# The first feed-forward layer of an encoder layer in two stages, with seven block products for eight

## The chip, the core and the metric

The kernel runs on one core of a Trainium2 chip. The metric is the device time in microseconds (us) of one execution. Three runs of the kernel before took 2439.05, 2436.93 and 2439.96 us, so the median is 2439.05 us. PE is the matrix engine, PEld its weight loads, DVE the vector engine, ACT the activation engine, POOL the general engine, SP the engine whose queue issues the transfers.

## The reference

One layer works on 1280 tokens of width 1024 in fp32: 256 of a prompt and 1024 of a sample.

```python
def swiglu(h, w_gu, w_down):
    gate, up = jnp.split(h @ w_gu, 2, axis=-1)
    return (jax.nn.silu(gate) * up) @ w_down

x = x + 0.5 * rms_norm(swiglu(rms_norm(x, ffn1_pre_g), ffn1_w_gu, ffn1_w_down), ffn1_post_g)
x = x + rms_norm(mixer(rms_norm(x, mix_pre_g), w_in, ..., w_out), mix_post_g)
x = x + 0.5 * rms_norm(swiglu(rms_norm(x, ffn2_pre_g), ffn2_w_gu, ffn2_w_down), ffn2_post_g)
x = rms_norm(x, final_g)
```

`w_gu` is 1024 x 5632 (gate and up of 2816 columns each), `w_down` is 2816 x 1024. The mixer (a projection `w_in`, dilated attention, a depthwise convolution, `w_out`) is not touched by the change.

## The kernel before, in words

**Tiles.** Tokens stand in ten blocks of 128: 0 to 7 are the sample, 8 and 9 the prompt. Blocks are grouped in three tiles (`TILES`, L27): t=0 and t=1 of 512 tokens, t=2 of 256. The normed tokens are kept transposed in `hT[t]`, as a high and a low fp32r part (`hTth`, `hTtl`); every weight is split likewise by an ACT copy and a DVE subtraction (`whi`/`wlo` at L90 and L91, `wb` at L114 and L115, `wd` and `ahl` at L637 and L638). `mm3` (L196 to L200) makes one product out of three matmuls: high x high, high x low, low x high. So all matmuls bear the lines L198, L199 and L200, and are told apart by their tiles. The 2816 hidden columns are 22 slices f of 128.

**First layer** (`ffn`, L340, names `psgu`, `ah`, `al`, `psd`, `y`). For each f and each tile, `gu` (L344) makes gate and up: 2 x 8 x 3 matmuls into two banks `psgu`, then silu and product (L370, L371) and the split of the result into `ah` and `al` (L372, L373). `dn` (L376) multiplies that slice with its 128 rows of `w_down` at once: 2 x 3 matmuls for each block, and DVE adds the two banks `psd` to the block's sum `y` in SBUF (L390; for f=0 ACT copies, L388). The last two slices go through `dn2` (L393, adds at L407). The matmuls of f=0 are cut into chunks of 256 tokens.

**Second layer** (from L1281; `ffn_gu` L488, `ffn_down` L597). Stage one: slices 0 and 1 as before (`gu`, L496), the remaining 20 by `pair` (L518). There gate and up of the sample are one 2 x 2 block product (gate and up on one side, the two halves of the contraction on the other, two tiles on the third), made of seven block products in place of eight (`for i in range(8)`, L528; the eighth step belongs to the prompt alone, in bank `psR`): 7 x 4 x 3 matmuls of 512 tokens into the banks `psAB` and `psC`, and 4 x 4 x 3 of 256 for the prompt. Its weights are sums of weight blocks (`Pairs`, L99: POOL adds at L134 to L140, then the split), and its tokens are sums of `hT` blocks (`token_sums`, L440: tiles `T2` to `T4`, and the first half of `hT1` overwritten), made once by DVE during slices 0 and 1. The gated activations `ac` go to DRAM (`ad`, L494). Stage two: `ffn_down` reads them back (`ar`, L620), splits them, and works in segments of (1, 3, 3, 3, 3, 3, 2, 4) slices: for each of ten blocks the matmuls of all slices of the segment run into `psd`, and the sum is added to the block (L667) once a segment (first segment: copies, L663 and L665). Weights of `w_down` are `wd`, loaded into the tag `g`.

**Behind each layer** the `chain` (L234) runs for each block in five steps, one at each call of `step` (L284): the sum of squares (ACT L206, POOL L207 and L208), scaling (DVE L212) and the residual (POOL L254), spill to DRAM (L263) and the second sum of squares, scaling (DVE L212 into `tmp`), transposes (PE L223) and the split into `hT` (ACT L225, DVE L226). For the first layer it feeds `w_in` (L684), whose first products are `psa`, `psb` (two column groups for each tile: 24 matmuls of each for a tile) and, behind them, `psqk`.

**Order.** Each engine works its queue in order. The order of the program is set by a scheduler that places the instructions by a time model, so that work of neighbouring steps is interleaved; all transfers are issued from SP's queue. Rings of buffers are set by tags: ten buffers `w` of 4 KB for split weights (L1197), two `raw`, two each of `x`, `tmp`, `g`, four PSUM banks of tag `g`, two double banks of tag `d`.

Of the kernel before, what the change touches and what calls it, by code (L numbers as in the profile page):

```python
# [10 lines left out]
F32 = mybir.dt.float32  # L11
# [87 lines left out]
class Pairs:  # L99
# [5 lines left out]
    def load(self, f, s):  # L105
        if f < NF and (f, s) not in self.raw:
            raw = self.t.wp.tile([P, D], F32, name="raw", tag="raw", bufs=2)
            c = s * FF + f * P
            self.t.nc.sync.dma_start(raw.rearrange("p (k m) -> p k m", k=KT), self.wgu[:, :, c:c + P])
            self.raw[f, s] = raw  # L110
# [38 lines left out]
class Trunk:  # L149
# [157 lines left out]
    def first(self, y, gname):  # L307
        nc = self.nc
        g = []
        V = {}  # L310

        def load(b0, b1):
            for b in range(b0, b1):
                nc.sync.dma_start(y[b], self.rows(self.a["x_prompt"], self.a["x_sample"], b))

        def s1(b):
            V[b] = self.rstd(y[b], self.tmp("tmp" if b % 2 else "x"), 1.0)

        def s2(b):
            self.scaled(y[b], y[b], V.pop(b), g[0])  # L320

        def s3(b):
            self.to_hT(b, y[b])

        load(0, 2)
        g.append(self.gain(gname))
        load(2, 4)
        return load, (s1, s2, s3)


    def ffn_units(self, w_gu, w_down):
        wgu = w_gu.rearrange("(k p) f -> p k f", p=P)
        units = []
        for f in range(NF):
            units.append((wgu[:, :, f * P:(f + 1) * P], (KT, P), None))
            units.append((wgu[:, :, FF + f * P:FF + (f + 1) * P], (KT, P), None))
            units.append((w_down[f * P:(f + 1) * P, :], (D,), None))
        return units

    def ffn(self, pool, S, base, y, done, prep=None, order=(0, 1, 2)):  # L340
        nc = self.nc
        act = {}

        def gu(f, t):  # L344
            n = TILES[t][1] * P
            if f == 0:
                self.ensure(t)
            hh, hl = self.hT[t]
            ps = []
            for s in range(2):  # L350
                o = self.bank("psgu")
                wh, wl = (z.rearrange("p (k m) -> p k m", k=KT) for z in S.w[base + 3 * f + s])
                for c0 in range(0, n, 256 if f == 0 else n):
                    c = slice(c0, c0 + 256 if f == 0 else n)
                    for k in range(KT):
                        self.mm3(o[:, c], (wh[:, k], wl[:, k]), (hh[:, k, c], hl[:, k, c]), k == 0, k == KT - 1)
                ps.append(o)
                if s == 0 or t < 2:
                    self.step()
            S.conv_to(base + 3 * f + 4 + t)  # L360
            tag = "c" if t == 2 else ""
            s = pool.tile([P, 512], F32, name="sg", tag="sg", bufs=1)
            if f == NF - 1:
                tag = ""
            if f == NF - 1 and t == 0:
                ah, al = self.tmp("x", (P, n), F32R), self.tmp("tmp", (P, n), F32R)
            else:
                ah = pool.tile([P, n], F32R, name="ah", tag="ah" + tag, bufs=1 if tag else 2)
                al = pool.tile([P, n], F32R, name="al", tag="al" + tag, bufs=1 if tag else 2)
            nc.scalar.activation(s[:, :n], ps[0][:, :n], AF.Silu)  # L370
            nc.vector.tensor_tensor(s[:, :n], s[:, :n], ps[1][:, :n], op=OP.mult)  # L371
            nc.scalar.activation(ah, s[:, :n], AF.Copy)  # L372
            nc.vector.tensor_tensor(al, s[:, :n], ah.bitcast(F32), op=OP.subtract)  # L373
            act[f, t] = ah, al

        def dn(f, t):  # L376
            dh, dl = S.w[base + 3 * f + 2]
            ah, al = act.pop((f, t))
            b0, nb = TILES[t]
            for j in range(nb):  # L380
                o = self.two_banks("psd")
                bl = slice(j * P, (j + 1) * P)
                for h in range(2):
                    c = slice(h * 512, (h + 1) * 512)
                    self.mm3(o[:, c], (ah[:, bl], al[:, bl]), (dh[:, c], dl[:, c]), True, True)
                yb = y[b0 + j]
                if f == 0:
                    nc.scalar.activation(yb, o, AF.Copy)  # L388
                else:
                    nc.vector.tensor_tensor(yb, yb, o, op=OP.add)  # L390


        def dn2(f, t):  # L393
            d = [S.w[base + 3 * g + 2] for g in (f - 1, f)]
            x = [act.pop((g, t)) for g in (f - 1, f)]
            b0, nb = TILES[t]
            for j0 in range(0, nb, 2):
                o = [self.two_banks("psd") for _ in range(2)]
                for i in range(2):
                    for j in range(2):  # L400
                        bl = slice((j0 + j) * P, (j0 + j + 1) * P)
                        for h in range(2):
                            c = slice(h * 512, (h + 1) * 512)
                            self.mm3(o[j][:, c], (x[i][0][:, bl], x[i][1][:, bl]), (d[i][0][:, c], d[i][1][:, c]), i == 0, i == 1)
                for j in range(2):
                    self.step()
                    nc.vector.tensor_tensor(y[b0 + j0 + j], y[b0 + j0 + j], o[j], op=OP.add)  # L407

        L = NF - 1
        for f in range(L):  # L410
            if f == 3 and prep:
                prep()
            if f == 0 and order[0] == 2:
                for t in order:
                    gu(0, t)
                dn(0, 0)
                dn(0, 1)
                continue
            gu(f, 0)
            if f:  # L420
                dn(f - 1, 2)
            gu(f, 1)
            if f < L - 1:
                dn(f, 0)
            gu(f, 2)
            if f < L - 1:
                dn(f, 1)
        for t in range(3):
            gu(L, t)
            dn2(L, t)  # L430
            done(t)

# [53 lines left out]
    def ffn_gu(self, pool, tpool, S, W, ad, orders, prep=None):  # L488
# [79 lines left out]
        def post(f, t, z, s):  # L568
            n = 2 * f + 3 + (z > 0)
            if n <= len(S.units):  # L570
                S.conv_to(n)
            elif z or s:
                W.to(1 if first else 3)
            if t == 1 and not T:
                t_, a_, b_ = self.token_sums(tpool)
                T.update(t_)
                first.extend(a_)
                then.extend(b_)
            if first:
                first.pop(0)()  # L580
            elif then and 1 in gone:
                then.pop(0)()
# [11 lines left out]
            pair(f)  # L594


    def ffn_down(self, ad, w_down, segs):  # L597
        nc = self.nc
        X, Wd, raw = {}, {}, {}
        c0 = [sum(segs[:s]) for s in range(len(segs) + 1)]  # L600
# [43 lines left out]
        def go(y, done):  # L644
            n0 = npre
            for s, n in enumerate(segs):
# [3 lines left out]
                for b in range(NB):  # L650
                    t = min(b // 4, 2)
                    k = n0 + -(-(n1 - n0) * (b + 1) // NB)
                    conv_to(k)
                    o = self.two_banks("psd")
                    j = (b - TILES[t][0]) * P
                    for c in cs:
# [525 lines left out]
def run(self):  # L1182
# [9 lines left out]
    def pool_(name, **kw):  # L1192
        m = tc.tile_pool(name=name, reuse_waits="tile", **{"bufs": 1, **kw})
        p = m.__enter__()
        return p, lambda: m.__exit__(None, None, None)

    wp, wp_x = pool_("wp", bufs=10, side="right")  # L1197
    self.wp = wp
    units = self.ffn_units(a["ffn1_w_gu"], a["ffn1_w_down"])
    b_in = len(units)  # L1200
    units += self.w_in_units()
    S = Stream(self, units)

    fy, fy_x = pool_("fy")
    fa, fa_x = pool_("fa", side="right")
    y = [fy.tile([P, D], F32, name=f"y{b}") for b in range(NB)]
    load, self.stages = self.first(y, "ffn1_pre_g")
    self.ready = list(range(NB))
    S.load_to(2)
    load(4, NB)  # L1210
    for _ in range(4):
        self.step()
    S.conv_to(1)
    self.ensure(0)
    S.conv_to(2)
    gp = self.gain("ffn1_post_g")
    gn = self.gain("mix_pre_g")

    def done1(t):
        if t == 0:  # L1220
            self.stages = self.chain(lambda b: y[b], xin, 0.5, gp, gn, spill=x2d)
        self.ready += range(TILES[t][0], sum(TILES[t]))

    def prep():
        z = self.tmp("tmp", (16, AW))
# [10 lines left out]
            nc.tensor.transpose(ps[:, j * (CK + 3):(j + 1) * (CK + 3)], cw[:, j * P:(j + 1) * P], self.ident[:CK + 3, :CK + 3])  # L1236
        nc.vector.tensor_copy(cv.rearrange("p j k -> p (j k)"), ps[:, 0:4 * (CK + 3)])

    self.ffn(fa, S, 0, y, done1, prep)
    fa_x()  # L1240
    wg, wg_x = pool_("wg", side="right")
    L = {}

# [3 lines left out]
        L["wc"], L["wc_x"] = pool_("wc")  # L1247
        return L["wc"]

    cacc = self.w_in(wg, conv_pool, S, b_in, qd, kd, vd, cv)  # L1250
    wg_x()
    wp_x()
    for t in range(3):
# [64 lines left out]

    self.place = place
    pre, go = self.ffn_down(ad, a["ffn2_w_down"], (1, 3, 3, 3, 3, 3, 2, 4))  # L1320
    self.ffn_gu(fa, ft, S2, Pairs(self, a["ffn2_w_gu"], 2, pre), ad, ((2, 0, 1), (1, 0, 2)))
    ft_x()
    fa_x()
    pools["p"], p_x = pool_("p2")
# [45 lines left out]
```

## Time and profile before

| | |
|---|---|
| median of three runs | 2439.05 us (2436.93 to 2439.96) |
| the profiled execution's own time | 2438.86 us |
| its span, first to last instruction | 2437.1 us |
| mean granted clock of PE over the span | 0.982 |
| DVE, ACT, POOL busy | 52%, 30%, 20% |
| first layer: first gate matmul, last down matmul | 18.1, about 949 us |
| second layer: first gate matmul, last down matmul | 1555.3, 2417.6 us |
| moved by DMA | 194.92 MB, mean 80 GB/s |

The span is the time from the first to the last instruction, and some 1.8 us of the execution lie around it. In the rows of the profile, a group is one line of the code with its output and input tiles, `x352` is the count, then come the busy time and the mean duration in ns. [...] In a row of the timeline, the number in brackets is how long the engine stood idle before it, with what ended the wait.

### The profile page before, as it was taken

The numbers are of one execution on the slowest core, as the hardware profiler recorded it, in microseconds if no ns is written. First come the engines' busy times: TensorE is split into PE (matmuls) and PEld (weight loads), VectorE is DVE, ScalarE is ACT, GpSimd is POOL, SyncE is SP. The second block draws the span as 40 slices with busy tenths as digits, with TensorE's granted clock in tenths as the row PEclk, the third lists the DMA queues.
The fourth block names the chain that finished last, engine by engine and source line by source line (L and its number), as shares of the span: only waits on it lengthen the run. The fifth ranks groups of instructions, "written<-read, shape, count | busy, mean of one in ns | idle before, by whom it ended". The sixth has DMA issues, their size and how long they took to land.

```text
span 2437.1 us, 30173 instructions
## 1 busy us (share of the span) xinstructions
PE 2350.7 (96%) x12028; PEld 2009.4 (82%) x12028; DVE 1263.2 (52%) x1695; ACT 739.9 (30%) x1387; POOL 491.5 (20%) x474
## 2 busy tenths in 40 slices
PE   7999999999999998999997799999999999999996
PEld 7888888888888887888886678888888888788885
DVE  5344444444444438899455553564344444454557
ACT  5211111111111125565356552332322222312113
POOL 2000000000000016797202233223232323100004
PEclk9999999999999999999998899999999999999998
DMA  5111111111111115241267552211222222432324
GB/s 179 44 35 44 35 44 35 44 35 44 35 44 35 44 61 164 70 124 61 78 157 148 112 157 95 93 57 61 72 70 68 74 62 84 130 106 68 106 74 154
DMA packets 191827, 194.92 MB, mean 80 GB/s; under 512 B 30212, under 2 KB 154916, under 8 KB 191686
## 3 DMA queue, kind: packets, MB, share of 16 engines
q1 hardware_dynamic: 191686, 193.00, 26.8%
q8 instruction: 94, 1.54, 0.3%
q14 instruction: 47, 0.39, 0.1%
HBM read 149.23 MB, written 43.73 MB: 79 GB/s over the span
## 4 chain that ended last, share of the span: by engine, by line
PE 87%; DMA 5%; DVE 3%; ACT 2%; issue 1%; POOL 1%; SPq 1%; POOLq 0%; ACTq 0%; DVEq 0%
PE psgu L198 9%; PE psgu L199 9%; PE psgu L200 9%; PE psd L198 7%; PE psd L199 7%; PE psd L200 7%; PE psAB L198 4%; PE psAB L199 4%; PE psAB L200 4%; PE psR L199 2%; PE psR L200 2%; PE psR L198 2%; PE psC L198 2%; PE psC L199 2%; PE psC L200 1%; PE psqk L198 1%
## 5 line engine op out<-in xcount | busy, mean ns | idle before, releaser
L390 DVE TENSOR_TENSOR y<-y,psd 128x1024 f32<-128x1024 f32 x190 | 231.6, 1219 | 176.2 <-PE psd L200 176.2
L207 POOL TENSOR_SCALAR st<-st 128x1 f32<-128x1 f32 x70 | 41.7, 596 | 1253.4 <-ACT tmp L206 981.8
L371 DVE TENSOR_TENSOR sg<-sg,psgu 128x512 f32<-128x512 f32 (+1 forms) x66 | 39.5, 599 | 273.0 <-PE psgu L200 273.0
L198 PE MATMUL psd<-wd,ahl 128*128 128x512 f32 x440 | 172.1, 391 | 3.3 <-DVE yh0l L663 1.4
L199 PE MATMUL psd<-wd,ahl 128*128 128x512 f32 x440 | 171.3, 389 | 0.0
L200 PE MATMUL psd<-wd,ahl 128*128 128x512 f32 x440 | 171.2, 389 | 0.0
L198 PE MATMUL psd<-whi,ah 128*128 128x512 f32 x432 | 169.7, 393 | 0.8 <-DVE y L407 0.8
L199 PE MATMUL psd<-wlo,ah 128*128 128x512 f32 x432 | 169.3, 392 | 0.0
L200 PE MATMUL psd<-whi,al 128*128 128x512 f32 x432 | 167.7, 389 | 0.0
L90 ACT ACTIVATE whi<-raw 128x1024 fp32r<-128x1024 f32 x98 | 103.2, 1058 | 212.1 <-PE psgu L199 166.9
L198 PE MATMUL psgu<-hT0h,whi 128*128 128x512 f32 (+1 forms) x416 | 155.9, 375 | 0.0
L198 PE MATMUL psgu<-hT1h,whi 128*128 128x512 f32 (+1 forms) x416 | 155.3, 373 | 0.5 <-ACT hT1h L225 0.5
L199 PE MATMUL psgu<-hT0l,whi 128*128 128x512 f32 (+1 forms) x416 | 155.6, 374 | 0.0
L200 PE MATMUL psgu<-hT0h,wlo 128*128 128x512 f32 (+1 forms) x416 | 155.4, 374 | 0.0
L91 DVE TENSOR_TENSOR wlo<-raw,whi 128x1024 fp32r<-128x1024 f32 x98 | 126.6, 1296 | 55.0 <-ACT whi L90 51.6
L199 PE MATMUL psgu<-hT1l,whi 128*128 128x512 f32 (+1 forms) x416 | 155.0, 373 | 0.0
L200 PE MATMUL psgu<-hT1h,wlo 128*128 128x512 f32 (+1 forms) x416 | 155.0, 373 | 0.0
L115 DVE TENSOR_TENSOR wb<-raw,wb 128x512 fp32r<-128x512 f32 x120 | 84.8, 708 | 106.4 <-ACT wb L114 103.9
L114 ACT ACTIVATE wb<-raw 128x512 fp32r<-128x512 f32 x120 | 75.5, 629 | 167.4 <-PE psC L200 68.0
L744 DVE SCALAR_TENSOR_TENSOR acc<-glu,cv,acc 128x1024 f32<-128x1024 f32 x96 | 121.5, 1284 | 1.8
L372 ACT ACTIVATE ah<-sg 128x512 fp32r<-128x512 f32 (+1 forms) x65 | 35.9, 553 | 253.0 <-DVE sg L371 253.0
L198 PE MATMUL psgu<-hT2h,whi 128*128 128x256 f32 x384 | 109.5, 286 | 2.8 <-DVE hT1l L226 2.8
(356 smaller groups left out, 6124.5 us busy)
## 6 DMA issues: line engine op xcount, KB each, us to landing
raw<-in_ffn_w_gu_dram SPq DMA_DIRECT2D x88, 512.0 KB
raw<-in_ffn_w_down_dram SPq DMA_DIRECT2D x22, 512.0 KB
ad<-ac SPq DMA_DIRECT2D x44, 256.0 KB
g<-in_ffn_w_down_dram SPq DMA_DIRECT2D x22, 512.0 KB
ar<-ad SPq DMA_DIRECT2D x44, 256.0 KB
raw<-in_w_in_dram SPq DMA_DIRECT2D x20, 512.0 KB
x2d<-y SPq DMA_DIRECT2D x10, 512.0 KB
q<-qd SPq DMA_DIRECT2D x16, 320.0 KB
```

The costliest lines, as they stand in the source:

```text
L90: nc.scalar.activation(hi, raw, AF.Copy)
L91: nc.vector.tensor_tensor(lo, raw, hi.bitcast(F32), op=OP.subtract)
L114: nc.scalar.activation(out[:, 0], src, AF.Copy)
L115: nc.vector.tensor_tensor(out[:, 1], src, out[:, 0].bitcast(F32), op=OP.subtract)
L198: mm(out, lh[0], rh[0], start=first, stop=False, skip_group_check=more)
L199: mm(out, lh[0], rh[1], start=False, stop=False, skip_group_check=more)
L200: mm(out, lh[1], rh[0], start=False, stop=last, skip_group_check=more)
L207: nc.gpsimd.tensor_scalar(st[:, 0:1], st[:, 0:1], 1e-6 / (mul * mul), None, op0=OP.add)
L371: nc.vector.tensor_tensor(s[:, :n], s[:, :n], ps[1][:, :n], op=OP.mult)
L372: nc.scalar.activation(ah, s[:, :n], AF.Copy)
L390: nc.vector.tensor_tensor(yb, yb, o, op=OP.add)
L744: nc.vector.scalar_tensor_tensor(V["acc"], gs(k), w(k), V["acc"], op0=OP.mult, op1=OP.add)
```

## The change

The first layer is computed by the functions of the second one. `ffn` and `ffn_units` are gone; `ffn_gu` and `ffn_down` are called for both layers. What differs from their use in the second layer:

- The prompt's blocks 8 and 9 are loaded first, and `gu(0, 2)` is the first product; tokens are loaded in the order 8, 9, (gain), 0, 1, then the first two weight slices, then blocks 2 to 7.
- Stage one has the tokens' tiles `y0` to `y9` in a pool `fy0` that is closed when the token sums are allocated (`tpool()`), so that `T2` to `T4` take their memory. The sums `y1` of stage two are in a new pool `fy`.
- The split `w_down` slices of a segment lie in the memory of `hT0` and `hT1` (free after stage one), in turn in two sets; of the last four slices, two lie in a pool `p1` and two in the memory of `hT2` (`where`, `place1`).
- `prep` (the convolution's constants) runs at the second pair.
- `also1` is called at each block of each segment: it loads the two gains after the last block but one segment, and in the last segment's blocks 7 to 9 loads and splits the first weights of `w_in`, which are now a stream of their own (`S_in`). `done1` appends each block to the chain at once in the last segment.
- The ring `w` has nine buffers.

```diff
-    def ffn(self, pool, S, base, y, done, prep=None, order=(0, 1, 2)):
...
-        load(0, 2)
+        load((8, 9))
         g.append(self.gain(gname))
-        load(2, 4)
+        load((0, 1))
...
-    def ffn_down(self, ad, w_down, segs):
+    def ffn_down(self, ad, w_down, segs, also=lambda s, b: None):
...
                     conv_to(k)
+                    also(s, b)
...
-    wp, wp_x = pool_("wp", bufs=10, side="right")
+    wp, wp_x = pool_("wp", bufs=9, side="right")
+    S = Stream(self, self.gu_units(a["ffn1_w_gu"], 2))
+    S_in = Stream(self, self.w_in_units())
+    ad1 = self.dp.tile([NF, P, NT], F32, name="ad1")
...
-    self.ready = list(range(NB))
+    self.ready = [8, 9, *range(8)]
     S.load_to(2)
-    load(4, NB)
+    load(range(2, 8))
...
-    gp = self.gain("ffn1_post_g")
-    gn = self.gain("mix_pre_g")
+    def tpool():
+        fy_x()
+        t, F["t_x"] = pool_("ft")
+        return t
...
-    self.ffn(fa, S, 0, y, done1, prep)
+    segs = (1, 3, 3, 3, 3, 3, 2, 4)
+    where = {}
+    c = 1
+    for i, n in enumerate(segs[1:-1]):
+        for z in range(n):
+            where[c] = ((("h0h", "h1h"), ("h0l", "h1l"))[i % 2][z // 2], z % 2)
+            c += 1
+    where |= {c: None, c + 1: None, c + 2: ("h2h", 0), c + 3: ("h2l", 0)}
+
+    def place1(c, what):
+        if what == "raw":
+            return self.tmp("g")
+        if c == 0:
+            return [self.wp.tile([P, D], F32R, name="wd", tag="w") for _ in range(2)]
+        if where[c] is None:
+            w = F["p"].tile([P, 2, D], F32R, name="wd", tag="wd", bufs=2)
+        else:
+            tag, z = where[c]
+            if z == 0:
+                F[tag] = self.hp.tile([P, 1 if tag[1] == "2" else 2, 2, D], F32R, name=f"wd{tag}", tag=tag)
+            w = F[tag][:, z]
+        return [w[:, z] for z in range(2)]
+
+    def also1(s, b):
+        if s == len(segs) - 2 and b == 9:
+            F["g"] = self.gain("ffn1_post_g"), self.gain("mix_pre_g")
+        elif s == len(segs) - 1 and b >= 7:
+            S_in.load_to(2)
+            S_in.conv_to(b - 7)
+
+    def done1(b):
+        if b == 0:
+            self.stages = self.chain(lambda b: y1[b], xin, 0.5, *F["g"], spill=x2d)
+        self.ready.append(b)
+
+    self.place = place1
+    pre, go = self.ffn_down(ad1, a["ffn1_w_down"], segs, also1)
+    self.ffn_gu(fa, tpool, S, Pairs(self, a["ffn1_w_gu"], 2, pre), ad1, ((2, 0, 1), (1, 0, 2)), prep)
+    F["t_x"]()
     fa_x()
+    fy, fy_x = pool_("fy")
+    F["p"], p_x = pool_("p1")
+    y1 = [fy.tile([P, D], F32, name=f"y{b}") for b in range(NB)]
+    go(y1, done1)
+    p_x()
...
-    cacc = self.w_in(wg, conv_pool, S, b_in, qd, kd, vd, cv)
+    cacc = self.w_in(wg, conv_pool, S_in, 0, qd, kd, vd, cv)
```

More of the change, by code (lines that the diff above doesn't have):

```diff
@@ L310, in first, with load @@
         V = {}
-        def load(b0, b1):
-            for b in range(b0, b1):
+        def load(bs):
+            for b in bs:
                 nc.sync.dma_start(y[b], self.rows(self.a["x_prompt"], self.a["x_sample"], b))
@@ L323, in s3 @@
             self.to_hT(b, y[b])
-        load(0, 2)
+        load((8, 9))
         g.append(self.gain(gname))
-        load(2, 4)
+        load((0, 1))
         return load, (s1, s2, s3)
[L331 to L338, printed above, removed]
@@ L340, in ffn @@
-    def ffn(self, pool, S, base, y, done, prep=None, order=(0, 1, 2)):
[L341 to L431, printed above, removed]
@@ L574, in post @@
             if t == 1 and not T:
-                t_, a_, b_ = self.token_sums(tpool)
+                t_, a_, b_ = self.token_sums(tpool())
                 T.update(t_)
@@ L1195, in pool_ @@
         return p, lambda: m.__exit__(None, None, None)
-    wp, wp_x = pool_("wp", bufs=10, side="right")
+    wp, wp_x = pool_("wp", bufs=9, side="right")
     self.wp = wp
[L1199 to L1204, printed above, removed]
+    S = Stream(self, self.gu_units(a["ffn1_w_gu"], 2))
+    S_in = Stream(self, self.w_in_units())
+    ad1 = self.dp.tile([NF, P, NT], F32, name="ad1")
+    fy, fy_x = pool_("fy0")
     fa, fa_x = pool_("fa", side="right")
@@ L1207, in run @@
     load, self.stages = self.first(y, "ffn1_pre_g")
-    self.ready = list(range(NB))
+    self.ready = [8, 9, *range(8)]
     S.load_to(2)
-    load(4, NB)
+    load(range(2, 8))
     for _ in range(4):
         self.step()
-    S.conv_to(1)
-    self.ensure(0)
     S.conv_to(2)
-    gp = self.gain("ffn1_post_g")
-    gn = self.gain("mix_pre_g")
[L1219 to L1222, printed above, removed]
+    F = {}
+    def tpool():
+        fy_x()
+        t, F["t_x"] = pool_("ft")
+        return t
     def prep():
@@ L1320, in run @@
     pre, go = self.ffn_down(ad, a["ffn2_w_down"], (1, 3, 3, 3, 3, 3, 2, 4))
-    self.ffn_gu(fa, ft, S2, Pairs(self, a["ffn2_w_gu"], 2, pre), ad, ((2, 0, 1), (1, 0, 2)))
+    self.ffn_gu(fa, lambda: ft, S2, Pairs(self, a["ffn2_w_gu"], 2, pre), ad, ((2, 0, 1), (1, 0, 2)))
     ft_x()
```

## The prediction, made before the change was run

> **What bounds the kernel now.** I read the page first, for the engine that is busy all the time, then the busy time by stretches, then the rows of PE's timeline for the pace of its matmuls, then the waits.
>
> ```profile
> span 2437.1 us, 30173 instructions
> PE 2350.7 (96%) x12028; PEld 2009.4 (82%) x12028; DVE 1263.2 (52%) x1695; ACT 739.9 (30%) x1387; POOL 491.5 (20%) x474
> ...
> PE   7999999999999998999997799999999999999996
> ...
> PE 87%; DMA 5%; DVE 3%; ACT 2%; issue 1%; POOL 1%; SPq 1%; POOLq 0%; ACTq 0%; DVEq 0%
> ```
>
> PE is busy for 96% of the span and holds 87% of the chain that ended last. Of 40 slices of 61 us, the first layer fills the first 15, and there PE leaves room in the first slice and in the sixteenth. The stretches show that with numbers (columns: length, then busy us of PE, PEld, DVE, ACT and POOL with instruction counts, granted clock, DMA share, GB/s):
>
> ```profile
> 0.00:61.00 61.00, 47.77 (x344) 45.22 (x345) 34.13 (x40) 36.21 (x57) 15.46 (x29) 0.97 0.53 178
> 61.00:122.00 61.00, 61.00 (x294) 51.45 (x293) 21.18 (x25) 15.58 (x20) 0.00 (x0) 1.00 0.15 44
> ...
> 854.00:915.00 61.00, 61.00 (x297) 51.57 (x297) 23.80 (x23) 13.60 (x23) 8.67 (x11) 1.00 0.20 64
> 915.00:976.00 61.00, 52.98 (x268) 44.60 (x267) 55.15 (x47) 30.80 (x54) 37.93 (x44) 0.92 0.51 161
> 976.00:1037.00 61.00, 60.33 (x320) 51.86 (x321) 51.67 (x50) 35.05 (x60) 43.80 (x39) 0.97 0.23 74
> ...
> 1647.00:1708.00 61.00, 61.00 (x328) 52.87 (x327) 25.56 (x38) 16.82 (x30) 18.71 (x13) 1.00 0.19 61
> 2074.00:2135.00 61.00, 58.00 (x284) 47.47 (x283) 30.19 (x39) 22.38 (x32) 4.65 (x3) 1.00 0.43 134
> ```
>
> The rows from 61 to 915 us are the first and the last of fourteen in which PE is full at its full clock: the first layer takes exactly the time of its matmuls. Then comes a stretch, from 915 to 1037, in which the first layer's chain hands over to the mixer's projection and DVE is as good as full (55.15 of 61): PE idles 8.0 + 0.7 us, and the clock falls short by 8% and 3% of 61 us, 6.7 us at the most. I call these 8.7 + 6.7 = 15.4 us the handover's loss. The row at 1647 lies among the pairs of the second layer, the very code that the first layer is to have: PE full, DVE at 42%, POOL at 31%. The row at 2074 holds the second layer's passage to its down products.
>
> **The pace of a matmul.** Three neighbouring groups of one slice f in PE's timeline (their first rows):
>
> ```profile
> 863.12 0.39 PE L198 MATMUL psgu<-hT1h,whi 128*128 128x512 f32 x1
> ...
> 874.00 0.28 PE L198 MATMUL psgu<-hT2h,whi 128*128 128x256 f32 x1
> ...
> 879.75 0.40 PE L198 MATMUL psgu<-hT0h,whi 128*128 128x512 f32 x1
> ```
>
> Gate and up of one tile are 48 matmuls. Those of 512 tokens take 874.00 - 863.12 = 10.88 us, so 0.2267 us each; those of 256 tokens 5.75 us, so 0.120 each. [...]
>
> **The change, part by part.**
>
> *Stage one, the pairs.* Per slice, gate and up now are 2 x 48 = 96 matmuls of 512 tokens and 48 of 256: 96 x 0.2267 + 5.75 = 27.51 us. A pair has 7 x 4 x 3 = 84 and the same 48: 84 x 0.2267 + 5.75 = 24.79. The difference is 12 x 0.2267 = 2.72 us, and over 20 slices **54.4 us** leave PE. Whether the pairs keep that pace is seen in the second layer:
>
> ```profile
> 1614.92 0.40 PE L198 MATMUL psAB<-hT0h,wb 128*128 128x512 f32 x1
> ...
> L200 PE MATMUL psd<-wd,ahl x440: 387/389/397, 2107.5 to 2417.6; 128*128 128x512 f32 x147
> ```
>
> The first row starts its first pair; the second is one of three lines of its down matmuls (count, duration, first and last start). Counted, 20 pairs are 495.8 us, and 3 x 440 down matmuls 299.2, together 795.0. They took, with 0.2 for the last one, 2417.8 - 1614.9 = 802.9. So the form that is copied here costs 7.9 us over its count, where the old loop costs nothing over it. Part of that is seen where the down products begin and end (start, duration, and in brackets PE's idle time before it and what ended that):
>
> ```profile
> 2129.40 0.50 PE L198 MATMUL psd<-wd,ahl 128*128 128x512 f32 x1 [1.45 <-DVE yh0l L663]
> ...
> 2412.25 0.50 PE L198 MATMUL psd<-wd,ahl 128*128 128x512 f32 x1 [0.59 <-DVE yh0l L667]
> ```
>
> In the first segment a block has only 6 matmuls (1.36 us) for PE and a whole copy out of the banks for DVE or ACT, beside the splits of the next weights; PE waits for the copies. The same order comes to the first layer. About 1 us of the 7.9 belongs to the last blocks, which I book with the handover: **-6.9 us** here; bounds -5 (this segment's gaps are shared better, since the new weights lie in memory free before the sums are) and -12 (the slots of `hT1` come free only after the last pair's sixth product).
>
> *The down products.* The matmuls stay: 6 for each slice and block, 1320 in all. What goes is DVE's addition after every slice:
>
> ```profile
> L390 DVE TENSOR_TENSOR y<-y,psd 128x1024 f32<-128x1024 f32 x190 | 231.6, 1219 | 176.2 <-PE psd L200 176.2
> ```
>
> 190 additions become 70, but DVE waited for PE here (176.2 us), so this is worth nothing to the time. The round trip by DRAM (66 stores of `ac`, 66 loads of `ar` and their splits) lies beside full PE in the row at 1647, DMA at 19%; I cost it at nothing. Without that cover each of the 66 splits would cost at most the 1.22 us that DVE takes above for twice the elements, so up to 80 us.
>
> *The start.* Today:
>
> ```profile
> 18.05 0.56 PE L198 MATMUL psgu<-hT0h,whi 128*128 128x256 f32 x1
> ...
> 40.80 1.28 DVE L226 TENSOR_TENSOR hT1l<-psT,hT1h 128x512 fp32r<-128x512 f32 x2
> ```
>
> Five transfers of 512 KB stand ahead of the weights as before (two token blocks, the gain, two more), so the first product can begin no more than a microsecond earlier, after two blocks in place of four. What today fills PE between the tiles, `dn` of slice 0, is no longer there, so PE meets DVE's work on later blocks sooner; and the token sums come on top. In the second layer they stand between these rows:
>
> ```profile
> 1571.16 2.35 DVE L462 TENSOR_TENSOR x<-hT1h,hT0h 128x1024 f32<-128x1024 f32 x2
> ...
> 1607.19 2.31 DVE L450 TENSOR_TENSOR T4l<-tmp,T4h 128x1024 fp32r<-128x1024 f32 x1
> ```
>
> That is 1609.5 - 1571.2 = 38.3 us. The sample's last transposed blocks are split by 42.1 us (the row at 40.80), so the sums can end at 42.1 + 38.3 = 80.4. Slice 0 runs in chunks of 256 tokens, 2 x 5 x 24 matmuls, slice 1 in whole tiles: 240 x 0.120 + 27.51 = 56.3 us of PE, with 4 us of today's gaps and transposes about 60 from 17.5 on: the first pair begins near 78 to 83 and needs the last sum `T4` only as its seventh product, 6 x 2.72 + 2 x 1.44 = 19 us later. It just fits. **0 us**; bounds +2 and -6 (the early sums late by as much as two of DVE's splits of 1.2 us for each of the two halves).
>
> *The handover.* The last segment gives PE 24 matmuls for each block, 5.44 us, plus 8 transposes of 128 tokens, which I estimate at 0.1 each from the 0.120 of a matmul of 256: 6.2 us. The chain starts with block 0 of that segment, so DVE's chain work is spread over ten such steps and 2 x 10.88 us of the projection's first tile. Today it starts only with the last slices, and DVE is full for two stretches. What DVE does for a block: one addition (1.22), two scalings, two splits (1.28, the row at 40.80), and a share of the eight activation splits of the segment (0.8 x 0.64 = 0.5). The scalings are of two kinds:
>
> ```profile
> 961.84 3.41 DVE L212 SCALAR_TENSOR_TENSOR tmp<-y,st,g 128x1024 f32<-128x1024 f32 x1 [0.77 <-POOL st L208]
> ...
> 980.29 1.29 DVE L212 SCALAR_TENSOR_TENSOR tmp<-y,st,g 128x1024 f32<-128x1024 f32 x1 [1.08 <-POOL st L208]
> ...
> 961.77 2.39 POOL L254 TENSOR_TENSOR y<-y,x 128x1024 f32<-128x1024 f32 x1
> ```
>
> The same instruction takes 1.29 alone, and 3.41 if POOL's residual addition began just before it. So DVE needs 1.22 + 1.29 + 1.28 + 0.5 = 4.3 and 1.3 or 3.4: 5.6 or 7.7 us for a block, against PE's 6.2. If all collide, DVE falls behind by 1.5 us for each of blocks 4 to 9, 9 us, of which the double bank and the projection's first tile hide a part. I take a loss of 6 where today is 15.4: **+9.4 us**; bounds +15.4 and 0.
>
> [...]
>
> PE's clock is the other half: in today's handover one gap is long.
>
> ```profile
> 920.02 1.97 PE L223 MATMUL psT<-ident,tmp 128*128 128x128 f32 x8 [3.83 <-DVE tmp L212]
> ```
>
> After this gap of 3.83 us the clock is down (0.92), while the gap of 1.45 us at 2129 left it at 1.00 (the stretch from 2074). My 6 us are such short gaps and carry no clock loss; one gap as at 920 would add up to 4.
>
> *The projection's ring* of nine buffers in place of ten: four weight slices live take eight, so one prefetch is later by one split (1.2 us) where PE has a block of 5.4 us. Nothing; bounds 0 and -2.
>
> **Sum.** 54.4 - 6.9 + 0 + 9.4 = 56.9 us off the profiled execution of 2438.86 (span 2437.1 and 1.8 around it): 2382.0. The median of 2439.05 lies 0.2 higher, which changes nothing: **2382 us**.
>
> **Rivals.**
>
> *The handover gains nothing* (DVE is the bound of the last segment, with all collisions and one long gap): loss 15.4, time 2382 + 9.4 = 2391. For it: DVE at 55 of 61 today, and the same chain. Against: it is spread over a longer stretch.
>
> *The first pair waits for the sums* (DVE ends at 95 in place of 80, being held by POOL's weight sums as in the rows of 2.31 above): 2382 + 10 = 2392. For it: no slack in the sum above. Against: `T4` has 19 us more.
>
> *Slower: the pairs wait for their weights.* A pair takes two loads of 512 KB into two `raw` buffers, which come free only when POOL's sums and the splits have read them. POOL already waits for them:
>
> ```profile
> POOL g L134 <- DMA raw<-in_ffn_w_gu_dram: 66.5, 19, 12.1
> ```
>
> 3.5 us in each of 19 pairs. PE pays only when the four of eight blocks that are split ahead (24.79 / 2 = 12 us) are used up. Each microsecond beyond that costs 20 us; from 2.85 us of waiting in every pair the gain is gone, and at 3.5 the kernel is at 2382 + 70 = 2452. Against it: PE stands at 61.00 of 61 in the row at 1647 with the same loads and buffers, DMA at 19%.
>
> *The change does not do what it says* would be a pair with 96 matmuls' time: gain 0, so 2382 + 54.4 = 2436. The row at 1614.92 and its stage speak against it.
>
> **How the numbers follow.** The forecast has 0.66, the handover rival 0.18, the late sums 0.10, the slower rival 0.04, and 0.02 a gain within 0.2% (5 us, about what a measurement of this kernel can tell from no change), where the weight waits eat just the gain. So faster 0.94, same 0.02, slower 0.04. The range: the good bounds together (handover +6.0, start +2, down +1.9) give 2372; the handover at nothing (9.4) with the down bound (5.1) gives 2396.5. I take **2372 to 2396**.
>
> **What would show it.** Gate and up of slices 2 to 21 as `psAB`, `psC`, `psR` with 24.8 to 24.9 us for a pair, so that the first layer's pairs span about 497 us from near 80; PE at 61 of 61 there. The handover, now between 915 and 1037, comes some 50 us earlier, and everything behind it by 57. DVE's L390 gone, L667 with 70 more. The handover's gaps under 2 us. I am wrong if PE waits for `wb` in the pairs, if the first pair starts after 90, or if the last segment takes over 75 us in place of 62.

## The result and the profile after

Four runs of the changed kernel took 2392.03 to 2396.55 us, median 2392.60; four of the kernel before in the same session took 2436.15 to 2439.96, median 2437.99. The ratio is 0.9817, with a 95% interval of 0.980 to 0.9834: the changed kernel is faster by 1.8%, or 45.4 us where 57 were forecast. 2392.6 lies in the range, in its upper half. In the profiled executions the span falls by 2437.1 - 2390.2 = 46.9 us.

The page of the changed kernel, the lines that answer to those of before:

```profile
span 2390.2 us, 30540 instructions
PE 2298.5 (96%) x11788; PEld 1965.1 (82%) x11788; DVE 1269.1 (53%) x1796; ACT 810.6 (34%) x1530; POOL 643.1 (27%) x574
...
PE   7999999999999999999978889999999999999996
...
PE 85%; DMA 5%; DVE 3%; issue 2%; ACT 2%; POOL 1%; SPq 1%; POOLq 0%; ACTq 0%; DVEq 0%
```

PE is still the bound and its 240 matmuls are gone from the count. Its busy time fell by 52.2 us and the span by 46.9, so some 5 us more than before are idle. The stretches show where (length, busy us of PE, PEld, DVE, ACT, POOL with counts, granted clock, DMA share, GB/s); the two from 868.3 lie as far before the first `psqk` as those from 915 did:

```profile
0.00:61.00 61.00, 43.90 (x293) 41.80 (x294) 35.83 (x42) 29.27 (x49) 14.98 (x28) 0.94 0.48 153
61.00:122.00 61.00, 61.00 (x342) 53.35 (x341) 46.32 (x51) 23.35 (x34) 21.94 (x12) 1.00 0.20 62
868.30:929.30 61.00, 55.26 (x266) 45.27 (x265) 55.62 (x51) 31.84 (x55) 37.70 (x43) 0.97 0.51 164
929.30:990.30 61.00, 61.00 (x331) 52.98 (x330) 43.25 (x41) 32.83 (x57) 38.44 (x36) 1.00 0.21 65
579.00:640.00 61.00, 56.19 (x251) 44.83 (x250) 31.20 (x36) 19.44 (x27) 1.69 (x1) 1.00 0.38 121
```

By the measure of the prediction (idle time of PE plus the missing clock) the start loses 17.1 + 3.7 = 20.8 us where it lost 13.2 + 1.8 = 15.0 before, and the handover 5.7 + 1.8 = 7.5 where it lost 15.4. The last row is the passage from the pairs to the down products: 4.8 us idle.

The pairs keep their pace. Two groups of PE (count, least/median/greatest duration in ns, first and last start), and the row of the first `psAB` product:

```profile
L198 PE MATMUL psAB<-T2h,wb x80: 389/389/389, 97.5 to 572.8; 128*128 128x512 f32 x80
...
L198 PE MATMUL psC<-hT1h,wb x4: 389/392/396, 94.7 to 96.8; 128*128 128x512 f32 x4
...
50.08 0.48 PE L198 MATMUL psAB<-hT0h,wb 128*128 128x512 f32 x1
```

The first group has four matmuls in each pair, three matmuls apart (a row lasts 389 ns, and the matmul behind it starts 0.2267 us after it does); from the first pair to the last are 572.8 - 97.5 - 9 x 0.2267 = 473.3 us, 24.91 for a pair, 0.12 over the count of 24.79. The second shows the first `psC` product at 94.7. Of the first pair, 12 matmuls of 0.2267 (`psAB`) and 12 of 0.120 (`psR`) come before it, 4.2 us of work. The scheduler put the 12 of `psAB` far ahead, at 50.08, in slice 0 before its last tile. Counted as if they stood with their pair, the first pair begins at 90.5.

### The profile page after: what moved, and what is told of

It is laid out like the page before. It is cut to its first block, busy times and chain, and to the rows that moved or that the text cites. A ratio compares the mean times of both kernels' runs of the same rounds, so it can differ in the third digit from the quotient of the medians.

```text
span 2390.2 us, 30540 instructions
## 1 busy us (share of the span) xinstructions
PE 2298.5 (96%) x11788; PEld 1965.1 (82%) x11788; DVE 1269.1 (53%) x1796; ACT 810.6 (34%) x1530; POOL 643.1 (27%) x574
## 4 chain that ended last, share of the span: by engine, by line
PE 85%; DMA 5%; DVE 3%; issue 2%; ACT 2%; POOL 1%; SPq 1%; POOLq 0%; ACTq 0%; DVEq 0%
PE psAB L198 8%; PE psAB L199 8%; PE psAB L200 8%; PE psd L198 7%; PE psd L199 7%; PE psd L200 7%; PE psR L199 3%; PE psR L200 3%; PE psR L198 3%; PE psC L198 3%; PE psC L199 3%; PE psC L200 3%; PE psgu L198 2%; PE psgu L199 2%; PE psgu L200 2%
## 5 line engine op out<-in xcount | busy, mean ns | idle before, releaser
L115 DVE TENSOR_TENSOR wb<-raw,wb 128x512 fp32r<-128x512 f32 x240 | 167.2, 698 | 217.5 <-ACT wb L114 212.8
L199 PE MATMUL psR<-hT2l,wb 128*128 128x256 f32 x640 | 181.1, 283 | 0.0
L200 PE MATMUL psR<-hT2h,wb 128*128 128x256 f32 x640 | 180.9, 283 | 0.0
L198 PE MATMUL psR<-hT2h,wb 128*128 128x256 f32 x640 | 180.5, 282 | 0.0
L198 PEld LDWEIGHTS psR<-hT2h,wb 128*128 128x128 f32 x640 | 122.2, 191 | 6.1
L199 PEld LDWEIGHTS psR<-hT2l,wb 128*128 128x128 f32 x640 | 122.2, 191 | 4.7
L198 PE MATMUL psAB<-hT0h,wb 128*128 128x512 f32 x320 | 125.7, 393 | 0.0
L198 PE MATMUL psC<-hT1h,wb 128*128 128x512 f32 x320 | 125.5, 392 | 0.0
L199 PE MATMUL psAB<-hT0l,wb 128*128 128x512 f32 x320 | 125.4, 392 | 0.0
L199 PE MATMUL psC<-hT1l,wb 128*128 128x512 f32 x320 | 125.4, 392 | 0.0
L200 PE MATMUL psAB<-hT0h,wb 128*128 128x512 f32 x320 | 124.5, 389 | 0.0
L200 PE MATMUL psC<-hT1h,wb 128*128 128x512 f32 x320 | 124.5, 389 | 0.0
L200 PEld LDWEIGHTS psR<-hT2h,wb 128*128 128x128 f32 x640 | 122.2, 191 | 1.6
L565 DVE TENSOR_TENSOR y<-y,psd 128x1024 f32<-128x1024 f32 x70 | 85.3, 1218 | 71.2 <-PE psd L200 71.2
```

Source lines behind the costliest of these rows:

```text
L115: nc.vector.tensor_tensor(out[:, 1], src, out[:, 0].bitcast(F32), op=OP.subtract)
L198: mm(out, lh[0], rh[0], start=first, stop=False, skip_group_check=more)
L199: mm(out, lh[0], rh[1], start=False, stop=False, skip_group_check=more)
L200: mm(out, lh[1], rh[0], start=False, stop=last, skip_group_check=more)
L565: nc.vector.tensor_tensor(y[b], y[b], o, op=OP.add)
```

## The experiments

All kernels below are the changed one with the edit shown, so line numbers behind an edit move by a few. "First psC" ends the start, "last psAB" the pairs (590.7 in the changed kernel), "first psqk" the handover (967.3).

**Why the start is late.** PE's rows with idle time in the changed kernel, then what DVE did then (start, duration; in brackets the idle time before and what ended it):

```profile
15.63 0.58 PE L198 MATMUL psgu<-hT2h,whi 128*128 128x256 f32 x1 [1.54 <-ACT whi L90]
...
29.84 1.26 PE L223 MATMUL psT<-ident,y 128*128 128x128 f32 x8 [2.71 <-DVE ac L412]
33.37 1.12 PE L223 MATMUL psT<-ident,y 128*128 128x128 f32 x4 [2.27 <-DVE hT0l L226]
```

```profile
24.08 1.28 DVE L212 SCALAR_TENSOR_TENSOR y<-y,st,g 128x1024 f32<-128x1024 f32 x1 [0.46 <-POOL st L208]
26.12 1.28 DVE L212 SCALAR_TENSOR_TENSOR y<-y,st,g 128x1024 f32<-128x1024 f32 x1 [0.75 <-POOL st L208]
28.17 1.28 DVE L212 SCALAR_TENSOR_TENSOR y<-y,st,g 128x1024 f32<-128x1024 f32 x1 [0.77 <-POOL st L208]
29.37 0.41 DVE L412 TENSOR_TENSOR ac<-ac,psgu 128x256 f32<-128x256 f32 x1
29.70 0.68 DVE L226 TENSOR_TENSOR hT0l<-psT,hT0h 128x512 fp32r<-128x512 f32 x1
30.30 1.28 DVE L212 SCALAR_TENSOR_TENSOR y<-y,st,g 128x1024 f32<-128x1024 f32 x1
31.50 1.22 DVE L91 TENSOR_TENSOR wlo<-raw,whi 128x1024 fp32r<-128x1024 f32 x1
32.63 1.28 DVE L226 TENSOR_TENSOR hT0l<-psT,hT0h 128x512 fp32r<-128x512 f32 x2
```

The prompt's tile is done first, and it is the short one: its 48 matmuls would last 5.8 us at the pace above, and with transposes between them and a slower pace at the start (0.21 us apart from 18.7 to 22.1) they end near 25.8. Then PE needs the product that frees its banks (L412, which ends the first gap) and the next splits (L226, which end the second). They stand in DVE's queue behind scalings of later blocks, three of which waited for POOL, and behind a weight split (L91). What stands in that queue is taken in order: L412 had its last matmul by 25.8 and its silu by 24.1, and DVE still stood idle for the 0.77 us ahead of the scaling at 28.17. The gaps cost more than their length: behind them the granted clock is 0.50 from 32.5 to 39.3, and matmuls of 256 tokens start 0.21 us apart in place of 0.12. Two runs separate this from a shortage of banks, and from the mere absence of `dn` as a filler.

*More banks*: the transposes of the start go to the double banks that the down products use later.

```diff
+        w = self.two_banks("psT") if self.wide else None
         for i in range(2):
-            ps = self.bank("psT").rearrange("p (k m) -> p k m", k=4)
+            ps = (w[:, 512 * i:512 * i + 512] if self.wide else self.bank("psT")).rearrange("p (k m) -> p k m", k=4)
```

> Until the down products begin, a block's transposes go to one of the two double banks (psd) instead of two of the four banks that gate and up also use. Theory A (PE waits at the start for a bank that the prompt's gate and up hold until DVE, busy with the scalings of later blocks, reaches their product): the two gaps of 2.71 and 2.27 us at 29.8 and 33.4 us go and with them the low clock behind them, some 7 us together; the first product in psC starts at 88 in place of 94.7, and the time falls by 6 to 2386. Theory B (DVE's own work and order bound the start, the bank only shows it): PE then waits for hT0l instead, psC first starts at 92 to 95, the time within 2 us of 2392.6.

Measured: 2392.17 us, ratio 0.980 (0.9781 to 0.9818), first psC at 91.7 with a first product 2.0 us earlier too (13.6), so that from the first product to the first psC are 78.1 us where the changed kernel has 79.1, and the other profiles with its order 78.3 to 78.9. PE's row:

```profile
29.02 0.66 PE L225 MATMUL psT<-ident,y 128*128 128x128 f32 x4 [2.83 <-DVE hT0l L228]
```

The longest gap stays, with DVE's split as its end instead of DVE's product, and the stretch is at most 1.0 us shorter than in the others: banks were not the cause.

*The old order*: sample first, in loads, in the chain and in the tiles of slice 0.

```diff
-        load((8, 9))
+        load((0, 1))
         g.append(self.gain(gname))
-        load((0, 1))
+        load((2, 3))
...
-    self.ready = [8, 9, *range(8)]
+    self.ready = list(range(NB))
-    load(range(2, 8))
+    load(range(4, NB))
...
-    ad1, ((2, 0, 1), (1, 0, 2)), prep)
+    ad1, ((0, 1, 2), (1, 0, 2)), prep)
```

> The start as it was before the change: tokens loaded and prepared in the order 0 to 9, slice 0 in the tile order 0, 1, 2. Theory F (what is missing is the filler, the down products of slice 0, whatever the order): psC first starts within 3 us of 94.7, the time within 3 us of 2392.6. Rival (the prompt first, whose gate and up take only 5.8 us, is what lets PE run dry): psC first starts at 87 to 88, the time 2386.

Measured: 2387.93 us, ratio 0.9787 (0.9766 to 0.9807). Its first `psC` group and its first stretch:

```profile
L198 PE MATMUL psC<-hT1h,wb x8: 389/394/468, 87.6 to 98.2; 128*128 128x512 f32 x8
```

```profile
0.00:61.00 61.00, 48.61 (x343) 45.24 (x344) 50.02 (x54) 32.84 (x53) 20.04 (x29) 0.97 0.48 156
```

First psC comes 7.1 us earlier although the first product comes 2.6 later (18.2), PE's busy time in the stretch is back at that of before (47.77) and above, and the longest gap between products is 0.49. From the first product to the first psC are 69.4 us, and 69.1 to 69.4 in the three runs with this order. There is no `dn` here either, so the filler was not needed: with a first tile of 512 tokens PE does not run dry. Which part of the order does it (loads, chain or tiles) was not separated. Of the 7.1 us, 5.2 are left at the last psAB (a gap of 1.30 at the second product into psC of the first pair is new) and 5.0 at the first psqk. By time alone the gain over the changed kernel is not clear, as the two intervals overlap.

**What is left of the handover.** The chain's residual addition moves from POOL to DVE.

```diff
-                (nc.gpsimd if out is None else nc.vector).tensor_tensor(y, y, x, op=OP.add)
+                nc.vector.tensor_tensor(y, y, x, op=OP.add)
```

> The residual of the first layer's chain is added by DVE instead of POOL (1.22 us of DVE for 2.4 of POOL, ten times). Port theory (the scalings that take 3.41 us beside a POOL addition set the handover): they take 1.29, DVE's work for a block falls from 7.7 to 6.8 us, the loss of the handover falls from about 10 to 5 us, the time to 2388. Rival (DVE's amount of instructions sets it, the collisions fall into idle time): the handover grows by up to 10 x 1.22 us less what is hidden, the time 2394 to 2400.

Measured: 2385.26 us, ratio 0.9775 (0.9756 to 0.9794). The ten second scalings of the handover (least/median/greatest ns), first in the changed kernel:

```profile
L212 DVE SCALAR_TENSOR_TENSOR tmp<-y,st,g x10: 1271/3392/3414, 856.8 to 926.2; 128x1024 f32<-128x1024 f32 x10
```

then in this one, with the stretch of its handover:

```profile
L212 DVE SCALAR_TENSOR_TENSOR tmp<-y,st,g x10: 1276/1284/1287, 857.9 to 919.6; 128x1024 f32<-128x1024 f32 x10
```

```profile
868.30:929.30 61.00, 59.92 (x300) 49.99 (x299) 51.61 (x58) 32.22 (x54) 19.19 (x34) 1.00 0.50 164
```

DVE took on the chain's additions at 1.22 us each and still was busy for 4.0 us less in this stretch (51.61 for 55.62; over the whole execution 3.2 less, 1265.9 for 1269.1), because no scaling is stretched any more: six of the ten took 3.4 in the changed kernel. PE's idle time falls from 5.7 to 1.1 and the clock is full: 6.4 us of the 7.5 are gone, and first psqk is at 961.0. From the first down product of the last segment to the first psqk are 120.1 us, and 120.1 to 120.7 in the three runs with this edit; the changed kernel has 127.1 and the five other runs 127.3 to 127.6. So the handover gained 7 us. The trace of the changed kernel shows the collision from both sides: DVE's scaling takes 3.41 for 1.28 where POOL's addition began first, and POOL's addition takes 3.37 for 2.40 where DVE's scaling did (the scalings at 898.26 and 906.25, then the additions at 898.19 and 906.41):

```profile
898.26 3.41 DVE L212 SCALAR_TENSOR_TENSOR tmp<-y,st,g 128x1024 f32<-128x1024 f32 x1 [0.77 <-POOL st L208]
...
906.25 1.27 DVE L212 SCALAR_TENSOR_TENSOR tmp<-y,st,g 128x1024 f32<-128x1024 f32 x1
```

```profile
898.19 2.40 POOL L254 TENSOR_TENSOR y<-y,x 128x1024 f32<-128x1024 f32 x1
...
906.41 3.37 POOL L254 TENSOR_TENSOR y<-y,x 128x1024 f32<-128x1024 f32 x1 [2.74 <-DVE y L212]
```

**Where the gain comes from.** Two stages and the way by DRAM stay, but slices 2 to 21 are made with eight products.

```diff
-    S = Stream(self, self.gu_units(a["ffn1_w_gu"], 2))
+    S = Stream(self, self.gu_units(a["ffn1_w_gu"], NF))
...
+        if plain is not None:
+            for f in range(2, NF):
...
+                for z, t in enumerate((0, 1, 2)):
+                    gu(f, t, lambda s: post(f, t, z, s))
```

> The first layer stays in two stages, but slices 2 to 21 make gate and up as slices 0 and 1 do, with eight block products and no token or weight sums. By the counts of the prediction PE has 20 x 2.72 = 54.4 us more, less the 0.1 us by which a pair exceeds its count: the time is 2392.6 + 52 = 2445, above the kernel before (2438), because the two stages alone cost their passage to the down products and the start. Rival (the gain came from the two stages, for example from DVE's additions that went, and the seven products give less than their count): 2425 or less.

Measured: 2441.82 us (ten runs), ratio 1.0008 (0.9998 to 1.0017). First psqk:

```profile
L198 PE MATMUL psqk<-hT0h,whi x10: 389/389/396, 1015.1 to 1029.5; 128*128 128x512 f32 x10
```

Two stages alone are worth nothing in sum (the handover gains about what the start and the passage lose), and seven products for eight make the whole gain: 1015.1 - 967.3 = 47.8 us. Counted from the first product, which came at 14.2 here and at 15.6 in the changed kernel, it is 49.2, that is 5.2 less than the count of 54.4. The pairs' 0.12 over the count explains 20 x 0.12 = 2.4. The passage to the down products explains some 3 more: the first 60 down matmuls take 17.2 us here, and in the changed kernel 25.8, of which 24 matmuls of the last pair among them are 5.4.

*The way by DRAM, doubled*: each slab of activations is stored twice; nobody reads the second copy.

```diff
-            nc.sync.dma_start(ad[f, :, c:c + TILES[t][1] * P], a)
+            for z in (ad if isinstance(ad, tuple) else (ad,)):
+                nc.sync.dma_start(z[f, :, c:c + TILES[t][1] * P], a)
```

> Every slab of activations of the first layer (66 of them) is stored to DRAM a second time, into a copy that nobody reads; all else is the changed kernel. Theory 'the way by DRAM is hidden' (booked at 0): the pairs keep their 496 us from the first psC product to the last psAB product, and the time stays within 3 us of the changed kernel's 2392 to 2393. Rival 'the way by DRAM is on the path' (an ac or x buffer is free only after its store, and the loads of weights stand behind the stores in SP's queue): with twice the stores each of the 20 pairs would be later by at least 0.3 us, so the pairs take 502 us or more and the time is 2399 or more.

Measured: 2390.07 us, ratio 0.9794 (0.9779 to 0.9808). The stretch of the pairs, first in the changed kernel, then in this one:

```profile
94.00:590.00 496.00, 495.44 (x2630) 427.97 (x2629) 207.60 (x306) 141.15 (x243) 139.76 (x97) 1.00 0.24 77
```

```profile
94.00:590.00 496.00, 494.67 (x2622) 426.83 (x2620) 206.77 (x302) 140.81 (x242) 138.92 (x96) 1.00 0.32 103
```

DMA rises from 24% to 32% and the pairs stay at 496.0 us from first psC to last psAB (the second stretch holds 1.2 us of down products, as its start was earlier). Nothing of the stores is on the path. The way back (the loads of `ar` and their splits) was not changed, so this run does not show it.

**The passage to the down products.** In the changed kernel PE's longest wait there ends with a bank copy by ACT (L563), and ACT's rows show what the copy stood behind:

```profile
600.09 0.50 PE L198 MATMUL psd<-wd,ahl 128*128 128x512 f32 x1 [2.66 <-ACT y L563]
```

```profile
598.07 1.06 ACT L534 ACTIVATE wdh0l<-g 128x1024 fp32r<-128x1024 f32 x1 [5.32 <-DMA g<-in_ffn_w_down_dram]
599.03 1.01 ACT L563 ACTIVATE y<-psd 128x1024 f32<-128x1024 f32 x1
```

The split belongs to a weight that is needed only in the segment after the next; the scheduler put it ahead, and its load came late. In the run with doubled stores the same loads land at other times, and PE's wait moves with them: before the first two of these splits ACT waits 1.91 and 2.29 us where the changed kernel has 0.68 and 5.32, and PE's long wait (2.30) is for the copy behind the first split. So the three early splits went to POOL.

```diff
+                if u[0] == "w" and self.wide and u[1] in (4, 5, 6):
+                    nc.gpsimd.tensor_copy(hl[0], r)
+                    nc.gpsimd.tensor_tensor(hl[1], r, hl[0].bitcast(F32), op=OP.subtract)
+                else:
```

> The splits of the three down weights of the second-next segment (4, 5 and 6), which the scheduler put ahead of bank copies in ACT's and DVE's queues, are done by POOL in the first layer; all else is the changed kernel. Theory 'PE waits at the beginning of the down products because the copy stands behind a split that waits for its weight': the gaps of 1.16 and 2.66 us before psd products near 592 and 600 go to under 0.5 each, the first psa product comes some 3 us earlier (near 900.5), time near 2389 to 2390. Rival 'the first segment is bound by the pace of the copies or by the landing of weights': the gaps stay or move to other blocks of the segment, first psa within 1 us of 903.5, time 2391 to 2394; if POOL's work blocks DVE's copies as in the handover, later than that.

Measured: 2390.4 us, ratio 0.980 (0.9783 to 0.9817), as good as the 2390.07 of the doubled stores in the same session (the changed kernel itself did not run in it): no gain. The first psa is at 901.9 (903.5 in the changed kernel), but from the last psAB to the first down product of the last segment are 249.0 us, where the changed kernel has 249.5 and the doubled stores 248.2. DVE's and POOL's rows, and PE's:

```profile
591.41 2.78 DVE L540 TENSOR_TENSOR ahl<-ar,ahl 128x512 fp32r<-128x512 f32 x1
594.12 1.21 DVE L566 COPY y<-psd 128x1024 f32<-128x1024 f32 x1
```

```profile
590.92 2.73 POOL L537 TENSOR_TENSOR wdh0l<-g,wdh0l 128x1024 fp32r<-128x1024 f32 x1
```

```profile
595.38 0.50 PE L199 MATMUL psd<-wd,ahl 128*128 128x512 f32 x1 [1.77 <-DVE y L566]
```

The wait of 2.66 is gone, as the theory said, but a wait of 0.43 became 1.77: POOL's subtraction held off a DVE split that takes 0.69 elsewhere for 2.78, and the other copy came late behind it. Both readings were half right; by these rows DVE and POOL held each other up as in the handover (POOL's subtraction takes 2.73 here and 2.40 in the two later splits), and that took the gain.

**The cures together.** First the old order with the residual on DVE, then these two with the splits on POOL.

> The two cures together: the start in the order of the kernel before (e2_order) and the first chain's residual add on DVE (e3_dve_res). If the two losses lie in different places and each is real, they add: first psC product at 87 to 89 instead of 94.7, first psqk product at 956 to 958 instead of 967.3, span near 2380, time 2381 to 2383. Rival 'one of the two single gains was the scatter of its profile or came from the other's place': only one of them is left, first psqk near 962, time 2386 to 2388.

> All three cures: the start in the old order, the residual add on DVE, the three early splits on POOL. If all three losses are real and lie in different places: first psqk near 953 to 955, span near 2377, time 2378 to 2380, which would be about 0.975 of the kernel before. If the third is none: the same as with two, 2381 to 2383.

Measured: 2382.51 us, ratio 0.9761 (0.9745 to 0.9777), first psqk at 955.7; and 2380.30, ratio 0.9753 (0.9739 to 0.9768), first psqk at 951.1, span 2376.8. The second kernel's handover:

```profile
868.30:929.30 61.00, 59.92 (x298) 49.87 (x297) 43.54 (x49) 27.31 (x46) 16.73 (x30) 1.00 0.37 121
```

This stretch lies some 16 us later in its handover than in the changed kernel; from 830 on, PE has no other wait above 0.15 us than the 1.08 in it.

The two losses are real and lie in different places: 11.6 us earlier at the first psqk, where the single runs gave 5.0 and 6.3. The third cure brought 4.6 in the profile here, nothing by time when alone and 2.2 by time here, with overlapping intervals. From the last psAB to the last segment are 247.6 us with it, 251.2 with the two cures and 251.6 with the residual on DVE alone, but 248.2 to 249.7 in four runs with neither: whether it helps stays open. Both kernels beat the changed one; the intervals of the last, 0.9739 to 0.9768, and of the changed kernel, 0.980 to 0.9834, are apart.

## Why the prediction was right, and where not

**Sum.** Its terms were 54.4 - 6.9 + 0 + 9.4 = 56.9. By the profile they are 54.4 for the matmuls, -8.9 for the pairs' surplus and stage two, -5.8 (by the stretches) to -7.1 (by the old order) for the start, and +7.9 for the handover, which makes 46.3 to 47.6 against the 46.9 of the spans. The range held the time by luck in part: its upper end added the bounds of the handover and of stage two, 14.5 us, and not the start's bound of -6. The handover and stage two used up 3.5 of that, and the start's loss found its place in the rest.

**The pairs: right.** A pair takes 24.91 us where 24.8 to 24.9 were said, and PE is full from the first to the last. The kernel with eight products shows that the rest brings nothing in sum. The rival of pairs that wait for their weights has no support: the stretch of 496 us is 495.4 busy at full clock, with DMA at 24% as at 32%.

**The way by DRAM and DVE's 190 additions at nothing: right as far as tried.** For the stores of the first the doubled stores show it; the loads back and their splits were not tried alone. For the second speaks the kernel with eight products, which drops the additions too and is not faster; alone they were not tried either.

**Stage two, booked -6.9: right in kind, 2.0 too small.** The passage costs 6.5 us (the spacings of the 13 matmuls that stand further apart than their pace, from 587 to 608, are 9.4 us against 13 x 0.2267 = 2.9), and the pairs' 0.12 each 2.4. The passage is not the same in each run: with the doubled stores, whose down products are the same, that sum is 4.4. I took the second layer's surplus whole without asking what it consisted of. The cause of the longest gap is shown in ACT's queue; that it can be cured there is not.

**The start, booked 0 with a bound of -6: the step that failed.** It said that the first pair begins at 78 to 83 and that the sums just fit. By count it begins at 90.5, past the 90 that the prediction named as a sign of being wrong, and the loss against before is 5.8 by the stretches and 7.1 by the run with the old order. The sum counted PE's matmuls and DVE's last sum, and noted that "PE meets DVE's work on later blocks sooner", but gave that no price, since it did not walk DVE's queue: after the short first tile, the product and the split that PE needs stand behind scalings that take turns with POOL. The 60 us for slices 0 and 1 were short too: with the old order, from the first product at 18.2 to the first pair at 83.5 by count, they take 65.3. And the first product came 2.4 us earlier than before, where no more than 1 was said.

The rival in which the first pair waits for the sums gave the right time, 2392, for another reason. What it asked for did happen: the last sum ends at 94.1 in place of 80.4, with rows of 2.3 us in it, while with the old order it ends at 80.2.

```profile
91.78 2.32 DVE L347 TENSOR_TENSOR T4l<-tmp,T4h 128x1024 fp32r<-128x1024 f32 x1
```

But PE did not wait for it: from 34 to 580 us PE has no gap at all in the changed kernel.

**The handover, booked +9.4: 7.9 came.** A loss of 6 was taken from today's 15.4, and 7.5 was left; the last segment took 60.9 us (its down products start from 840.2 to 901.1) where 62 were said, and the gaps were 1.87 and 2.98 where under 2 was said. The reason given was the right one. The run with the residual on DVE shows that the collisions make nearly all of it (7.5 to 1.1). That the gaps would carry no clock loss was wrong: 1.8 of the 7.5 are the clock (0.97 in the stretch with the gap of 2.98). The rival in which the handover gains nothing falls. The loss of 9 that was worked out for a collision in every block, with nothing of it hidden, was on the high side; six of ten scalings collided. In the rows that the prediction shows, the scaling's 3.41 is roughly its 1.29 alone and the 2.32 that POOL's addition had left when that scaling began, a sum of 3.61. The rows of the changed kernel agree: there the one that began first holds the other up for about what is left of its own length (3.41 and 3.37 above).

**The ring of nine at nothing** was not tried alone. From 929.3 to 990.3, in the projection, PE is busy for 61.00 of 61, and no gap in the pairs ends with a weight split, so no loss is seen.

## What to carry to other kernels

When the order of the first loads is changed, walk the in-order queue of the engine that prepares the tiles, and ask what stands ahead of the first result that the matrix engine waits for; with the shortest tile first, the matrix engine started sooner here (15.6 for 18.1) and ran dry (idle for 2.71 and 2.27 us). DVE's scalings and splits and POOL's additions on whole blocks are not to be costed as if they ran side by side (3.41 for 1.28, 2.78 for 0.69): moving ten additions of 2.4 us from POOL to the fuller DVE gained 7 us at the handover, and moving three splits from ACT and DVE to POOL gained nothing by itself. When a form of code is copied from another layer, split its surplus into its parts before booking it.

## What the runs showed of the hardware beside that

Small POOL instructions were held up too (1.31 for 0.22). POOL's rows of the changed kernel's start show the same addition on 128 x 1 elements at two lengths:

```profile
20.85 0.22 POOL L207 TENSOR_SCALAR st<-st 128x1 f32<-128x1 f32 x1
...
24.13 1.31 POOL L207 TENSOR_SCALAR st<-st 128x1 f32<-128x1 f32 x1
...
26.17 1.31 POOL L207 TENSOR_SCALAR st<-st 128x1 f32<-128x1 f32 x1
```

The long ones begin 0.05 us after a scaling of 1.28 on DVE (24.08, 26.12) and last to just behind its end. So the result that POOL makes for the next block's scaling comes late, and that scaling waits 0.75 us for it: the two took turns here.

The first product began between 13.6 and 15.6 us in the runs that keep the new order, with the same instructions ahead of it, so a difference of 2 us between the absolute times of two profiles says nothing by itself. For that reason the lengths of stretches (from the first product, or from the last segment's first down product) stand beside the absolute times above. In the run with the residual on DVE, for one, the last psAB was already 1.3 us earlier, ahead of the edit's place, and the passage behind it 2.1 longer.
